# Low parts of the gates' weights: added from DRAM to the negated high part by a GpSimd transfer, instead of subtracted on VectorE

## The chip, the core and the metric

The kernel runs on one core of one Trainium2 chip. The metric is the device time of one execution in microseconds; the time of a kernel is the median of several executions. A core has one instruction queue for each engine, and each engine works its queue in order: PE (TensorE, matrix products, with PEld for the loading of the stationary operand), DVE (VectorE), ACT (ScalarE), POOL (GpSimd) and SP (SyncE, which here only issues transfers). Transfers are carried out by 16 DMA engines.

## What is computed

One layer of a decoder trunk on 512 positions of width 1024, all in float32. The lines below are cut from the reference; attention has three dilated groups, the RWKV-7 mixer has 16 heads of 64, and the feed-forward part has 2816 channels.

```python
h = rms_norm(x, norm1_w[l]) * (1.0 + sc1) + sh1
proj = h @ w_in[l]
att_in, rwkv_in, gate_in = jnp.split(proj, [ATT_IN, ATT_IN + RWKV_IN], axis=-1)
y_att = attention_mixer(att_in) @ w_att_out[l]
y_rwkv = rwkv7_mixer(rwkv_in, ...) @ w_rwkv_out[l]
g_att, g_rwkv = jnp.split(jax.nn.sigmoid(gate_in + b_gate[l]), N_BRANCHES, axis=-1)
x = x + gt1 * ((g_att * y_att + g_rwkv * y_rwkv) @ w_o[l])
h = rms_norm(x, norm2_w[l]) * (1.0 + sc2) + sh2
x = x + gt2 * conv_ffn(h, w_up[l], conv_w[l], conv_b[l], w_down[l])
```

The change touches `gate_in` alone: the last 2048 columns of `w_in` times h, for the two sets of gates.

## The kernel before

**Products.** A float32 matrix product is made of three products of reduced operands (type float32r): each operand is split into a high part, a rounded copy, and a low part, what is left after it. The sum holds high times high, high weights times low input, and low weights times high input. `body` (L1099) makes such a product for 128 columns of weights: kt steps of 128 rows (8 for `w_in`), three products in each. In step k the order is whi with hhi, whi with hlo, wlo with hhi, so the low part of the weights is first read by the third product. A body of eight steps therefore has 24 products of 128x512.

**Weights.** `weights` (L1125) makes the operands of one body: SP loads the 512 KB matrix to `raw`, ACT casts it to `whi` (L1136), DVE subtracts `whi` from `raw` into `wlo` (L1139) and gives `raw` back. There are two buffers of `raw` and two of `whi` and `wlo` (the room "w"), so the cast for a body waits until the body two back has run its last product.

**Gates.** `early_gate` (L1208) is called for 16 blocks of 128 columns (`gate_w`, L1775). Each is a body into the PSUM tile `pg`, followed by a tanh on ACT into `gs` (L1780) and a store of the result to DRAM (`gate_d`), from where it is read back in a later stage.

**Order.** The order on all five engines is fixed when the program is built. `Plan` (L50 to L113) collects tasks, each with an engine, an estimated duration, a priority, the tasks it depends on and the rooms (buffers) it takes and gives back. `run` then plays the plan with these estimates, and always starts the ready task with the lowest priority number on each engine. The engines afterwards follow this order, whatever the real durations are: an engine waits at its next instruction until its inputs are there. `lag` is a time that a task's users wait after the task itself has left its engine, for transfers.

**What stands around the gates.** The RWKV mixer works on four groups of four heads, numbered 0 to 3. Each group goes through two long stages. Its *inverse* inverts triangular blocks: a chain of small DVE operations on the tile `tt` (L1497, L1498, L1505 to L1508) with transposes (L1514, L1519), between which PE has a few `pe` products. Its *chain* runs eight steps over the sequence; in each, PE makes `xy`, ACT copies it to `xs`, PE makes `u`, ACT copies it to `uv`, PE updates, and DVE carries the state `mbd` (L1641), to which POOL has made the decayed state `mp` ahead (L1626). While group g's chain runs, group g+1 is projected (the products `r`, `k`, `v`, whose results are shifted by one position with the help of the ACT copy `sh`, L1147) and goes through its inverse. The products of the gates have the highest priority number of this stage, and so fill what is left between the other products. What fills the end of the last chain is the output product of the attention, `pa`, which opens (`close_pre`, L1079) after all gates are stored.

Of the kernel before, what the change touches and what calls it, by code (L numbers as in the profile page):

```python
# [12 lines left out]
AF = mybir.ActivationFunctionType  # L13
ALU = mybir.AluOpType
# [4 lines left out]
P = 128  # L19
S = 512  # L20
D = 1024
KD = D // P
# [95 lines left out]
C_, E_, W_, V_, I_, M_, S_, U_ = 0.0, 1.0, 2.0, 200.0, 200.15, 220.0, 1.0, 10.0  # L118
# [10 lines left out]
class Layer:  # L129
# [966 lines left out]
    def psx(self, s):  # L1096
        return self.pps.tile([P, 512], F32, tag="px", name=self.n(s), bufs=2)

    def body(self, name, src, kt, room, make, rhs, deps=(), take=(), late=(), last=None, weights=None):  # L1099


        nc, pl = self.nc, self.pl
        n = src.shape[1]
        o = self.bodies = self.bodies + 1
        d = {}
        if weights is None:
            t = self.weights(name, d, src, kt, lambda: self.halves_w(kt, n), W_ + o, deps, tuple(take), ("w",))
        else:
            d["w"], t = None, weights(d, W_ + o)

        def unit(k, j):
            if k == 0 and j == 0:
                d["pm"] = make()
            w, x = d["w"], rhs(k)
            self.mm(d["pm"], w[j // 2][:, k, :], x[j % 2], k == 0 and j == 0, k == kt - 1 and j == 2)
        ends = kt if last is None else last
        for k in range(ends):
            for j in range(3):
                t = pl.add("PE", 0.237, lambda k=k, j=j: unit(k, j), [t] + (list(late) if k + j == 0 else []) +
                           ([self.hk[k]] if j == 0 and rhs == self.hT else []),  # L1120
                           U_ + o, take=(room,) if k + j == 0 else (),
                           give=("w",) if last is None and k == kt - 1 and j == 2 else (), name=name)
        return t, d

    def weights(self, name, d, src, kt, make, prio, deps=(), take=(), buf=()):  # L1125

        nc, pl = self.nc, self.pl
        n = src.shape[1]
        us = kt * n / 1000

        def load():
            d["raw"] = self.load_w(src, kt, n)

        def hi():
            d["w"] = make()
            nc.scalar.copy(d["w"][0], d["raw"])  # L1136

        def lo():
            nc.vector.tensor_tensor(d["w"][1], d["raw"], d["w"][0], op=ALU.subtract)  # L1139
        t = pl.add("DMA", 1.6 * us, load, deps, prio, take=("raw",) + take, lag=2.2, name=name)  # L1140
        t = pl.add("ACT", 0.04 + us, hi, [t], prio, take=buf, name=name + " hi")
        return pl.add("DVE", 0.17 + us / 0.96, lo, [t], prio, give=("raw",), name=name + " lo")

    def shift(self, t, pm, mu, omu, out, take=(), give=(), rows=P, name="shift", deps=()):
# [63 lines left out]
    def early_gate(self, m):  # L1208

        nc, pl = self.nc, self.pl  # L1210
        t, d = self.body("gate", self.gate_w(m), KD, "mm", lambda: self.mmp("pg"), self.hT)

        def tanh():
            d["t"] = self.pp.tile([P, S], F32, tag="km", name=self.n("gs"))
            self.gate(m, d["t"], d["pm"])

        def store():
            self.gd[m] = self.dr.tile([P, S], F32, name=f"gate_d{m}")
            nc.sync.dma_start(self.gd[m], d["t"])
        t = pl.add("ACT", 0.7, tanh, [t, self.pre], E_, take=("km",), give=("mm",))  # L1220
        self.gdt[m] = pl.add("DMA", 0.8, store, [t], M_, give=("km",), lag=2.0, marks=("pre",), name="gate out")
# [916 lines left out]
```

## Time and profile before

| what | value |
|---|---|
| three runs | 1253.78, 1249.96, 1244.15 us; median 1249.96 us |
| the profiled execution's own time | 1247.44 us |
| its span in the profile | 1245.7 us |
| mean granted clock of TensorE in it | 0.984 |
| DMA | 139.39 MB, mean 112 GB/s |
| the chain of work that ended last | PE 82%, DVE 8%, DMA 5%, ACT 2% |

The profile is of one execution. Its page gives busy times of each engine, then the span cut into 40 equal slices of 31.1 us with the busy share of each in tenths, then groups of instructions. In a row, `L1139 DVE` is line and engine, `wlo<-raw,whi` the tile written and the tiles read (buffer numbers left out), and behind the bar stand busy us and mean ns of one. A row of the timeline gives the start in us, the duration, and in square brackets the idle time ahead of it with what ended it. The windows give busy us and the number of instructions of each engine in a stretch. An average over the whole program says little here, since the stages have different limits; the stretch from 410 to 730 us is the one with the inverses, the chains and the gates.

### The profile page before, as it was taken

To read this page: it belongs to the slowest core of one execution; us is meant where nothing else is said; L and a number is where in the kernel's file an instruction comes from. 1 tells how busy PE (TensorE), PEld (TensorE's weight loads), DVE (VectorE), ACT (ScalarE), POOL (GpSimd) and SP (SyncE) were. 2 spreads that over 40 slices of the span, in tenths; PEclk is the share of its full clock that TensorE was granted. 3 is DMA by queue.
4 is the path that set the end of the run, shared out by engine and by line. 5 is a ranking of instruction groups with operands and counts; after the bars stand their busy time and mean duration, and the time that the engine had idled before them with its cause. 6 is when DMAs were issued, how large, how long until landed. Compare 5 with 4: busy or idle time off the path is not lost.

```text
span 1245.7 us, 18047 instructions
## 1 busy us (share of the span) xinstructions
PE 1197.4 (96%) x7012; PEld 976.5 (78%) x7012; DVE 746.5 (60%) x1242; ACT 545.4 (44%) x981; POOL 118.2 (9%) x235
## 2 busy tenths in 40 slices
PE   4999999999999999999999799999999999999997
PEld 3788878888787877777787577788888888878886
DVE  6697862422678968536896844555556566552235
ACT  4484522523566373455445343334443434442133
POOL 4000000000001013030002222214100000000001
PEclk9899999999999999999999789999999999999999
DMA  9745871130333332322330424571133332323331
GB/s 316 242 143 163 274 235 49 46 85 1 92 99 88 97 89 77 110 60 82 92 105 26 146 79 132 174 219 34 56 97 96 90 102 85 102 87 116 102 119 68
DMA packets 168900, 139.39 MB, mean 112 GB/s; under 512 B 8849, under 2 KB 150251, under 8 KB 168815
## 3 DMA queue, kind: packets, MB, share of 16 engines
q1 hardware_dynamic: 168671, 137.98, 36.5%
q8 instruction: 55, 0.90, 0.3%
q14 instruction: 30, 0.25, 0.1%
q10 hardware_dynamic: 144, 0.26, 0.1%
HBM read 127.65 MB, written 10.56 MB: 111 GB/s over the span
## 4 chain that ended last, share of the span: by engine, by line
PE 82%; DVE 8%; DMA 5%; ACT 2%; issue 1%; SPq 0%; POOL 0%; POOLq 0%; DVEq 0%; ACTq 0%
PE u L148 23%; PE o L148 13%; PE v L148 7%; PE pg L148 7%; PE qk L148 6%; PE xy L148 4%; PE pr L148 3%; DMA araw<-in_w_ada_dram 3%; PE k L148 3%; PE pa L148 2%; PE r L148 2%; PE early L148 2%; PE po L148 2%; PE sc L148 1%; PE pt L151 1%
## 5 line engine op out<-in xcount | busy, mean ns | idle before, releaser
L194 DVE TENSOR_TENSOR wlo<-raw,whi 128x1024 fp32r<-128x1024 f32 x67 | 84.1, 1255 | 151.0 <-ACT whi L193 150.9
L148 PE MATMUL u<-h2lo,whi 128*128 128x512 f32 (+2 forms) x368 | 142.3, 387 | 0.0
L148 PE MATMUL u<-h2hi,whi 128*128 128x512 f32 (+2 forms) x368 | 142.3, 387 | 0.0
L148 PE MATMUL u<-h2hi,wlo 128*128 128x512 f32 (+2 forms) x368 | 142.2, 386 | 0.0
L1136 ACT CAST whi<-raw 128x1024 fp32r<-128x1024 f32 (+2 forms) x73 | 72.5, 993 | 130.2 <-PE qk L148 49.5
L193 ACT CAST whi<-raw 128x1024 fp32r<-128x1024 f32 x67 | 70.3, 1049 | 112.0 <-PE o L148 53.8
L1139 DVE TENSOR_TENSOR wlo<-raw,whi 128x1024 fp32r<-128x1024 f32 (+2 forms) x73 | 84.2, 1154 | 22.9 <-ACT whi L1136 22.7
L148 PEld LDWEIGHTS u<-h2hi,wlo 128*128 128x128 f32 x368 | 68.9, 187 | 15.7
L148 PEld LDWEIGHTS u<-h2lo,whi 128*128 128x128 f32 x368 | 68.9, 187 | 15.7 <-POOL h2lo L405 0.2
L148 PEld LDWEIGHTS u<-h2hi,whi 128*128 128x128 f32 x368 | 68.9, 187 | 15.5
L1983 DVE SCALAR_TENSOR_TENSOR u<-u,cols,u 128x511 f32<-128x511 f32 x88 | 65.6, 746 | 4.2 <-ACT u L1981 2.7
L148 PE MATMUL qk<-hhi,wlo 128*128 128x512 f32 x160 | 63.9, 400 | 0.0
L148 PE MATMUL qk<-hlo,whi 128*128 128x512 f32 x160 | 63.6, 397 | 0.0
L148 PE MATMUL qk<-hhi,whi 128*128 128x512 f32 x160 | 63.5, 397 | 0.0
L148 PE MATMUL o<-whi,fhi 128*128 128x512 f32 x144 | 56.1, 390 | 0.3 <-DVE u L1983 0.3
L148 PE MATMUL o<-wlo,fhi 128*128 128x512 f32 x144 | 56.0, 389 | 0.0
L148 PE MATMUL o<-whi,flo 128*128 128x512 f32 x144 | 56.0, 389 | 0.0
L148 PE MATMUL pg<-hhi,wlo 128*128 128x512 f32 x128 | 52.0, 406 | 0.0
L148 PE MATMUL pg<-hlo,whi 128*128 128x512 f32 x128 | 51.8, 405 | 0.0
L148 PE MATMUL pg<-hhi,whi 128*128 128x512 f32 x128 | 51.3, 401 | 0.0
L810 DVE CUSTOM_DVE_ANT_0 sm<-sc,m 128x256 f32<-128x256 f32 (+1 forms) x64 | 24.0, 405 | 37.6 <-PE sc L148 36.5
L347 DVE SCALAR_TENSOR_TENSOR acc<-araw,cols,acc 128x1024 f32<-128x1024 f32 x28 | 35.9, 1282 | 17.2 <-DMA araw<-in_w_ada_dram 17.1
(404 smaller groups left out, 2824.0 us busy)
## 6 DMA issues: line engine op xcount, KB each, us to landing
raw<-in_w_in_dram SPq DMA_DIRECT2D x62, 512.0 KB
raw<-in_w_up_dram SPq DMA_DIRECT2D x44, 512.0 KB
araw<-in_w_ada_dram SPq DMA_DIRECT2D x32, 512.0 KB
raw<-in_w_down_dram SPq DMA_DIRECT2D x22, 512.0 KB
araw<-in_w_ada_dram SPq DMA_DIRECT2D x32, 256.0 KB
wvraw<-in_w_in_dram SPq DMA_DIRECT2D x20, 256.0 KB
gate_d<-gs SPq DMA_DIRECT2D x16, 256.0 KB
gate<-gate_d SPq DMA_DIRECT2D x16, 256.0 KB
```

The costliest lines, as they stand in the source:

```text
L148: return self.nc.tensor.matmul(out, lhsT, rhs, start=start, stop=stop)
L151: self.nc.tensor.matmul(out, in_, self.ident[: in_.shape[0], : in_.shape[0]], is_transpose=True, start=start, stop=stop,)
L193: self.nc.scalar.copy(hl[0], raw)
L194: (lo_eng or self.nc.vector).tensor_tensor(hl[1], raw, hl[0], op=ALU.subtract)
L347: nc.vector.scalar_tensor_tensor(d["acc"], raw, ck, d["acc"], op0=ALU.mult, op1=ALU.add)
L810: nc.vector.tensor_tensor_reduce(d["sm", h][:, :wd], d["sc"][h][:, :wd], m[:, 256 - wd : 256] if gi == 0 else m[:, :wd], 1.0, 3.0e38, op0= ...
L1136: nc.scalar.copy(d["w"][0], d["raw"])
L1139: nc.vector.tensor_tensor(d["w"][1], d["raw"], d["w"][0], op=ALU.subtract)
L1983: nc.vector.scalar_tensor_tensor(u[:, d:], pu[:, : S - d], ch(c), u[:, d:], op0=ALU.mult, op1=ALU.add)
```

## The change

For the 16 gate bodies, and for them alone, the low part is made in another way. `raw` is given back as soon as the cast to `whi` is done. ACT then writes minus `whi` into `wlo`, and POOL issues a transfer that reads the same 512 KB of `w_in` from DRAM once more and adds them to what stands in `wlo`. The subtraction on DVE is gone for these bodies; the other bodies keep it. To the plan, the new ACT task costs what the cast costs, and the POOL task 1.5 us with a lag of 4.0 us.

```diff
@@ body
-    def body(self, name, src, kt, room, make, rhs, deps=(), take=(), late=(), last=None, weights=None):
+    def body(self, name, src, kt, room, make, rhs, deps=(), take=(), late=(), last=None, weights=None, added=False):
...
-            t = self.weights(name, d, src, kt, lambda: self.halves_w(kt, n), W_ + o, deps, tuple(take), ("w",))
+            t = self.weights(name, d, src, kt, lambda: self.halves_w(kt, n), W_ + o, deps, tuple(take), ("w",),
+                             added)
@@ weights
-    def weights(self, name, d, src, kt, make, prio, deps=(), take=(), buf=()):
+    def weights(self, name, d, src, kt, make, prio, deps=(), take=(), buf=(), added=False):
...
         t = pl.add("ACT", 0.04 + us, hi, [t], prio, take=buf, name=name + " hi")
+        if added:
+
+            pl.join([t], give=("raw",))
+            t = pl.add("ACT", 0.04 + us, lambda: nc.scalar.activation(d["w"][1], d["w"][0], AF.Copy, scale=-1.0), [t], prio,
+                       name=name + " neg")
+            return pl.add("POOL", 1.5, lambda: nc.gpsimd.dma_start(
+                d["w"][1], src.rearrange("(k p) f -> p k f", p=P), accum_op=ALU.add), [t], prio, lag=4.0, name=name + " lo")
         return pl.add("DVE", 0.17 + us / 0.96, lo, [t], prio, give=("raw",), name=name + " lo")
@@ early_gate
-        t, d = self.body("gate", self.gate_w(m), KD, "mm", lambda: self.mmp("pg"), self.hT)
+        t, d = self.body("gate", self.gate_w(m), KD, "mm", lambda: self.mmp("pg"), self.hT, added=True)
```

Since the plan is played with other tasks, the order on the engines changes in many places. Line numbers behind L1139 are 7 or 8 higher after the change. In the lists below a row is one instruction in the order of its engine (or several alike, "x4"), with the tile written and the tiles read, their buffer numbers, and the semaphores it waits for.

On ACT at the inverse of group 0, where the first gates are made, `whi_3812` is the high part for the first gate, `whi_3854` (after the change `whi_3856`) that for the second, and the two copies `sh` belong to the projections `r` and `v` of the next group. Before:

```order
L1136 CAST whi_3812<-raw_3668 128x1024 [waits DMAHW2_49,PE_49]
L1147 ACTIVATE sh<-r_3750,cols 128x512 [waits PE_49,Activation_49]
L1136 CAST whi_3854<-raw_3782 128x1024 [waits DMAHW0_49,PE_49]
L1147 ACTIVATE sh<-v_3810,cols 128x512 [waits DVE_49,PE_49]
L1136 CAST whi_3894<-raw_3841 128x1024 [waits DMAHW1_49,DVE_49,PE_49]
```

After:

```order
L1137 CAST whi_3812<-raw_3668 128x1024 [waits DMAHW2_49,PE_49]
L1155 ACTIVATE sh<-r_3750,cols 128x512 [waits PE_49,Activation_49]
L1146 ACTIVATE wlo_3813<-whi_3812 128x1024 [waits Activation_49]
L1137 CAST whi_3856<-raw_3782 128x1024 [waits DMAHW0_49,PE_49]
L1155 ACTIVATE sh<-v_3810,cols 128x512 [waits DVE_49,PE_49]
L1146 ACTIVATE wlo_3857<-whi_3856 128x1024 [waits Activation_49]
L1137 CAST whi_3905<-raw_3825 128x1024 [waits DMAHW1_49,PE_49]
```

The negations stand behind the copies `sh`, and the third cast no longer waits for DVE.

On POOL in the chain of group 0, two steps of the chain (`mp`) with the first operations of an inverse (`tt`) and of the normalization of a chain's output (`var`, `rs`, `yt`). Before:

```order
L1626 TENSOR_SCALAR mp_4400<-mbd_86,pc_3228 128x128 [waits DVE_49]
L1626 TENSOR_SCALAR mp_4400<-mbd_87,pc_3338 128x128
L1486 MEMSET tt_4418 128x512 [waits PE_49,Activation_49]
L1488 TENSOR_SCALAR tt_4418<-rn_4330,half 128x16 [waits Pool_49]
L1488 TENSOR_SCALAR tt_4418<-rn_4330,half 128x16
L1763 TENSOR_SCALAR var_4415<-var_4415 128x4 [waits DVE_49]
L1764 TENSOR_TENSOR rs_4453<-var_4415,mhalf 128x4 [waits Pool_49]
L1765 TENSOR_TENSOR yt_4328<-yt_4328,rs_4453 128x256 [waits Activation_49,Pool_49]
L1626 TENSOR_SCALAR mp_4475<-mbd_86,pc_3228 128x128 [waits DVE_49]
```

After:

```order
L1634 TENSOR_SCALAR mp_4411<-mbd_86,pc_3228 128x128 [waits DVE_49]
L1634 TENSOR_SCALAR mp_4411<-mbd_87,pc_3338 128x128
L1494 MEMSET tt_4432 128x512 [waits Activation_49]
L1496 TENSOR_SCALAR tt_4432<-rn_4300,half 128x16 [waits Pool_49]
L1496 TENSOR_SCALAR tt_4432<-rn_4300,half 128x16
L1148 DMA wlo_4422<-in_w_in_dram 128x8x128 [waits DMASW3_49,PE_49,Activation_49]
L1634 TENSOR_SCALAR mp_4484<-mbd_86,pc_3228 128x128 [waits DVE_49]
```

A gate's transfer now stands between two steps' `mp`, and waits for ACT's negation (and for an earlier transfer and PE).

On PE at the inverse of group 3, which runs beside the chain of group 2: `xy` and `u` belong to that chain, `pe` to the inverse, `pg` are gates, and `t` is a transpose of the chain's output. Before:

```order
L148 MATMUL xy_6652<-uv_6574,gt_5357 64x64 x4
L148 MATMUL u_6161<-xs_6663,gt_5357 64x64 x4
L148 MATMUL xy_6652<-uv_6574,gt_5357 64x64 x4
L148 MATMUL pe_6718<-lt_6408,gt_5848 32x32 x32
L148 MATMUL pe_6718<-tt_6435,lt_6408 32x32 x32
L151 MATMUL t_6808<-ident,yt_6233 128x128
```

After:

```order
L148 MATMUL pg_6579<-hhi,whi_6456 128x512
L148 MATMUL pe_6651<-lt_6309,gt_5757 32x32 x32
L148 MATMUL pg_6579<-hlo,whi_6456 128x512
L148 MATMUL pg_6579<-hhi,wlo_6457 128x512
L148 MATMUL pg_6690<-hhi,whi_6589 128x512
L148 MATMUL pg_6690<-hlo,whi_6589 128x512
L148 MATMUL pg_6690<-hhi,wlo_6590 128x512
L148 MATMUL pg_6690<-hhi,whi_6589 128x512
L148 MATMUL pg_6690<-hlo,whi_6589 128x512
L148 MATMUL pe_6651<-tt_6350,lt_6309 32x32 x32
```

Before, the gates were all done when this inverse came to its products; after the change the last two gates run around them. Between the first product of group 2's inverse and the first of group 3's, PE has 80 gate products before the change and 111 after it.

## What I expected, on record before the run

> **What bounds the kernel now.** I read the page's busy times and its 40 slices first, then the windows of the stretch in which the sixteen gate products run, then single instructions there.
>
> ```profile
> span 1245.7 us, 18047 instructions
> PE 1197.4 (96%) x7012; PEld 976.5 (78%) x7012; DVE 746.5 (60%) x1242; ACT 545.4 (44%) x981; POOL 118.2 (9%) x235
> PE   4999999999999999999999799999999999999997
> DVE  6697862422678968536896844555556566552235
> PEclk9899999999999999999999789999999999999999
> ```
>
> PE is full but for the start, the end and slice 23 (around 700 us), where its granted clock dips too. DVE has spare time on the whole, but is nearly full in a few slices. The windows of the stretch show which (columns: busy us and instructions of PE, PEld, DVE, ACT, POOL, then clock, DMA share, GB/s):
>
> ```profile
> 419.00:434.20 15.20, 15.05 (x67) 12.13 (x65) 14.64 (x23) 5.58 (x8) 0.00 (x0) 1.00 0.50 138
> 442.00:494.00 52.00, 52.00 (x432) 40.54 (x431) 35.62 (x84) 28.69 (x65) 13.28 (x26) 1.00 0.26 77
> 494.00:513.00 19.00, 19.00 (x204) 15.36 (x203) 15.95 (x23) 8.17 (x11) 3.52 (x3) 1.00 0.49 146
> 631.00:651.00 20.00, 20.00 (x206) 16.36 (x205) 19.32 (x27) 10.94 (x15) 0.66 (x1) 1.00 0.39 104
> 651.00:696.00 45.00, 44.43 (x367) 33.93 (x366) 31.06 (x76) 20.88 (x50) 11.94 (x24) 1.00 0.13 41
> 696.00:727.00 31.00, 21.47 (x238) 17.53 (x239) 23.04 (x40) 14.24 (x30) 4.81 (x7) 0.56 0.60 183
> ```
>
> The inverses (DVE's long chains) run in 419 to 434, 494 to 513, 631 to 651 and 680 to 707. In the first three PE is full, because gate products fill it; in the fourth the gate products are used up, PE does 21.47 us of work in 31 us, and the clock falls to 0.56. So a us taken from DVE is worth something only at 696 to 727. Everywhere else PE sets the pace, and what counts is whether a gate's weights are there when PE gets to them. The time after is therefore the time before, plus new PE waits, less what of that one gap is filled.
>
> **Removed and added work, by engine.**
>
> ```profile
> L1139 DVE TENSOR_TENSOR wlo<-raw,whi 128x1024 fp32r<-128x1024 f32 x28 | 34.2, 1221 | 9.0 <-ACT whi L1136 8.9
> L1136 ACT CAST whi<-raw 128x1024 fp32r<-128x1024 f32 x28 | 29.4, 1049 | 53.6 <-PE pg L148 21.9 <-PE k L148 13.7 <-PE r L148 7.7
> ```
>
> Sixteen subtractions of 1.221 us leave DVE: 19.5 us, none of it on PE's path but in the gap. Sixteen negations come to ACT. The nearest row is the cast of the same size, 1.05 us, so 16.8 us; ACT is busy 5.58 of 15.2 us and 28.69 of 52 in the windows above, so the load fits, and I cost it only as latency of the weights. Should that cover go, each negation could hold a chain's copy by up to 1.05 us. The raw buffer is given back after the cast instead of the subtraction, which lets SP's next load go some 1.2 us or more earlier; PE doesn't wait for raw, so that is worth nothing. DMA gets 16 x 512 KB more to read, in windows that are at most 0.6 busy.
>
> **The price of the accumulating transfer, D.** No row shows one, nor any transfer issued by POOL.
>
> ```profile
> 575.22 3.92 DMA raw<-in_w_in_dram
> L1764 POOL TENSOR_TENSOR rs<-var,mhalf 128x4 f32<-128x4 f32 x16 | 16.5, 1030 | 1.3
> L1875 POOL TENSOR_TENSOR gate<-gate,gate 128x512 f32<-128x512 f32 x8 | 11.2, 1403 | 45.0 <-DVE gate L1874 45.0
> ```
>
> The same matrix loaded plainly by SP takes 3.92 us to land. At 146 GB/s for a share of 0.49 (494 to 513) full DMA moves 298 GB/s, so the 512 KB take 1.76 us of it, and 2.16 us are fixed. Lower end: 3.92, if adding costs nothing and POOL issues as fast as SP; a gain over the plain load has no reason, since the same bytes come from the same place. Upper end: two plain transfers in a row and POOL's longest row of this size, 2 x 3.92 + 1.40 = 9.2. I take 2.16 + 2 x 1.76, since the tile is read as well as the matrix, plus 1.03 for POOL writing the request: D = 6.7, nearer the middle than either end.
>
> **New waits on PE.** Before, a gate's low part follows its high part on DVE. Now it is cast, negation and D, and the cast waits as before until PE has finished the body two back.
>
> ```profile
> 413.69 1.05 ACT L1136 CAST whi<-raw 128x1024 fp32r<-128x1024 f32 x1 [2.14 <-PE r L148]
> 414.64 0.68 ACT L1147 ACTIVATE sh<-r,cols 128x512 f32<-128x512 f32 x1
> 418.93 0.19 PEld L148 LDWEIGHTS pg<-hhi,whi 128*128 128x128 f32 x1
> 632.23 0.69 ACT L1147 ACTIVATE sh<-r,cols 128x512 f32<-128x512 f32 x1
> 631.29 5.44 PE v L148 x24
> 502.37 0.68 ACT L1780 ACTIVATE gs<-pg,b_gate 128x512 f32<-128x512 f32 x1
> 645.80 1.13 PE pe L148 x64
> 498.26 0.58 PE t L151 x4
> ```
>
> A body is 24 products in 5.44 us, 0.227 each; only its third product reads the low part, so 0.45 us of each wait is covered.
> (a) First gate at inverse 0. The negation stands behind the copy sh: it ends at 414.64 + 0.68 + 1.05 = 416.4, the transfer lands at 423.1, PE is free at 418.93: 4.2 - 0.45 = 3.7.
> (b) First gate at the third inverse (inverse 2), the same way: 632.23 + 0.69 + 1.05 + 6.7 = 640.7 against 636.73: 4.0 - 0.45 = 3.5.
> (c) Third gate at inverse 0: cast 1.05, tanh 0.68, negation 1.05, hops some 0.15, D, together 9.65, from the end of the first gate; PE has 24 products and two inverse products, 5.44 + 2 x 1.13 = 7.7: 1.9 - 0.45 = 1.5.
> (d) The last two gates of the first chain: 9.65 again, against 5.44 + 2.1 of chain products, and against 5.44 + 2 x 0.58: 1.6 and 2.6, together 4.2.
> In the chains a body lasts about 5.44 + 5 = 10.5 us, because a chain's own products stand between; 9.65 fits, so nothing there.
>
> **The gap, and what takes its place.**
>
> ```profile
> 706.42 0.71 DVE L1519 STREAM_TRANSPOSE lt<-tt 128x512 f32<-128x512 f32 x1
> 707.19 1.94 PE pe L148 x64
> 701.59 1.11 PE L148 MATMUL u<-xs,gt 64*64 64x64 f32 x8 [0.51 <-ACT xs L1621]
> 720.21 2.00 PE pa L148 x4
> 723.68 1.99 PE t L148 x4
> 688.53 0.68 PE L148 MATMUL u<-xs,gt 64*64 64x64 f32 x8
> ```
>
> Now about 31 more gate products (7.0 us) run after the third inverse, around the fourth one's products, and DVE has five subtractions less there. That fills 31 - 21.47 = 9.5 us of idle time. The clock stays up, too: two inverse products at 1.13 instead of 1.94 (1.6), pa and t x4 at 0.91 instead of 2.00 and 1.99 (2.2), and four groups of eight like u at 0.68 instead of 1.11 (1.7), about 6 after rounding up for smaller ones; it could be 0 or, at (1 - 0.56) x 21.47, 9.4. Gain: 15.5. Next is late the last chain: in its new order two steps stand with no other product between, and two nearly so.
>
> ```profile
> 686.80 0.67 PE L148 MATMUL xy<-uv,gt 64*64 64x64 f32 x8
> 687.57 0.37 ACT L1621 COPY xs<-xy 64x256 f32<-64x256 f32 x1 [2.33 <-PE xy L148]
> 689.24 0.37 ACT L1658 COPY uv<-u 64x256 f32<-64x256 f32 x1 [1.30 <-PE u L148]
> 684.52 0.61 DVE L1641 SCALAR_TENSOR_TENSOR mbd<-u,pc,mp 128x128 f32<-128x128 f32 x2
> 685.23 0.72 POOL L1626 TENSOR_SCALAR mp<-mbd,pc 128x128 f32<-128x128 f32 x2 [2.36 <-DVE mbd L1641]
> 692.23 0.61 DVE L1641 SCALAR_TENSOR_TENSOR mbd<-u,pc,mp 128x128 f32<-128x128 f32 x2 [1.20 <-ACT uv L1590]
> ```
>
> In a bare step PE waits for two copies and the carry, 0.37 + 0.37 + 0.61, and some six hops of 0.1, less the 0.67 us of its output products that fit in: 1.3. (e) 2 x 1.3 + 2 x 0.5 = 3.6.
>
> **Sum.** 3.7 + 3.5 + 1.5 + 4.2 + 3.6 - 15.5 = +1.0 us. The profiled execution took 1247.44 us (span 1245.7), 0.2% under the median of the three runs, 1249.96; added to the median: 1251.
>
> POOL's queue: six of its transfers stand ahead of an mp of a chain. mp ends at 685.95 and is read at 692.23, some 6 us later, so a hold of POOL below about 5 us is covered; the mp behind waits for the negation too.
>
> **Rivals.** They differ in D, whose slope is about 5 us per us.
> *Slow transfer, slower.* At D = 9.2: (a) 6.2, (b) 6.0, (c) 4.0, (d) 4.1 + 5.1, (e) 3.6, and four bodies in chains fall short by 12.15 - 10.5 - 0.45 = 1.2 each: 33.8 - 15.5 = +18, 1268. Over 1% slower from D = 8.4 on. For it: the transfer is of 512-byte pieces, two reads for one write. Against: DMA is at most half busy there.
> *Hidden transfer.* At D = 3.92: 0.9 + 0.7 + 0 + 0 + 3.6 - 15.5 = -10, 1240; with the last chain filled, too, -14, 1236, which is faster by over 1%. For it: the plain load. [...]
> *POOL held, slower.* If writing the request holds POOL for 7.5 us, six mp are late by 2.5 each, and D grows by as much as POOL is held beyond 1.03: over 1270, in any case. [...]
> *The relief isn't used.* If the gap stays as it is and the waits come on top: 16.5, 1266.
>
> **How the numbers follow.** About 1% is what a measurement of this kernel tells from no change (the three runs differ by 0.8%). My case, D from 4.5 to 8.4: 0.48. Hidden transfer: 0.16, of it 0.10 faster by over 1%. Slow transfer 0.25, POOL held 0.06, relief unused 0.05: slower 0.36. So faster 0.10, same 0.54, slower 0.36. Range: 1238 leaves out about 0.08 below; above, D could exceed my bound, and 1281 (about D = 11) leaves out 0.12.
>
> **What would show it.** Right: PE waits for wlo at its first gates of inverses 0 and 2 by 3 to 4 us each, the window of 31 us is full and its clock near 1, DVE has 19.5 us less, and the last chain shows gaps of half a us. Wrong: a wlo that lands over 8 us after POOL's issue, PE waits inside the chains, mp late, or the clock falling at the new waits.

## The result, and the profile after

The changed kernel takes 1255.75 us (median of 6 runs, 1255.32 to 1262.1) against 1249.1 us before: a ratio of 1.0064, 95% interval 1.0038 to 1.0090. It is slower by 0.6%, clear of the scatter but within the 1% that the prediction took as no change, and 4.75 us above the 1251 that was predicted. The profiled execution took 1255.35 us.

The page of the changed kernel, busy times and three of its rows of slices:

```profile
span 1253.6 us, 18111 instructions
PE 1202.6 (96%) x7012; PEld 978.1 (78%) x7012; DVE 726.2 (58%) x1226; ACT 560.3 (45%) x997; POOL 142.1 (11%) x251
PE   4999999999999899999989989999999999999997
DVE  6697862422678948436975745555555565552235
PEclk9899999999999999999989979999999999999999
```

DVE has lost its 20 us and ACT gained 15. The dip of PE and its clock that stood in slice 23 is gone; PE has new ones in slices 14, 21 and 24, the clock in the last two of them. The windows of the same stretches as before show them (busy us of PE, PEld, DVE, ACT, POOL, then clock, DMA share, GB/s):

```profile
419.00:434.20 15.20, 11.77 (x111) 9.30 (x110) 13.97 (x21) 8.22 (x12) 3.07 (x2) 1.00 0.93 159
494.00:513.00 19.00, 16.86 (x194) 12.69 (x192) 14.24 (x22) 8.67 (x13) 4.33 (x5) 1.00 0.70 153
631.00:651.00 20.00, 16.48 (x177) 12.78 (x176) 16.31 (x25) 8.09 (x11) 2.94 (x2) 0.83 0.70 121
696.00:727.00 31.00, 30.47 (x340) 23.65 (x338) 19.29 (x34) 15.41 (x33) 8.38 (x11) 1.00 0.36 76
727.00:773.00 46.00, 42.90 (x295) 33.80 (x294) 19.96 (x38) 20.96 (x48) 14.92 (x22) 0.81 0.49 148
```

The window of the fourth inverse, 696 to 727, is now full at full clock, as forecast. The first three inverses, which were full before, are now short of it by 3.4, 2.1 and 3.5 us of PE, and the last chain (727 to 773, 46.00 of 46 before) by 3.1 us and a fifth of its clock. The transfers, from the list of DMA issues (the last number is the median from issue to landing):

```profile
wlo<-in_w_in_dram POOLq DMA_DIRECT2D x16, 512.0 KB, 6.7
```

And from the instructions of their line (shortest, median and longest on POOL, in ns):

```profile
L1148 POOL DMA_DIRECT2D wlo<-in_w_in_dram x16: 1522/1600/1788, 416.8 to 703.8; - x16
```

The timeline has five waits of PE for a landing, and six waits in the last chain, of which two are shown; what ended the idle time stands in brackets:

```profile
423.36 0.50 PE L148 MATMUL pg<-hhi,wlo 128*128 128x512 f32 x1 [3.43 <-DMA wlo<-in_w_in_dram]
438.58 0.50 PE L148 MATMUL pg<-hhi,wlo 128*128 128x512 f32 x1 [1.34 <-DMA wlo<-in_w_in_dram]
495.82 0.50 PE L148 MATMUL pg<-hhi,wlo 128*128 128x512 f32 x1 [0.85 <-DMA wlo<-in_w_in_dram]
504.01 0.50 PE L148 MATMUL pg<-hhi,wlo 128*128 128x512 f32 x1 [1.02 <-DMA wlo<-in_w_in_dram]
637.32 0.79 PE L148 MATMUL pg<-hhi,wlo 128*128 128x512 f32 x1 [3.52 <-DMA wlo<-in_w_in_dram]
...
725.36 0.45 PE L148 MATMUL u<-uv,bkt 128*64 128x64 f32 x8 [0.46 <-ACT uv L1666]
730.45 0.68 PE L148 MATMUL u<-xs,gt 64*64 64x64 f32 x8 [1.22 <-ACT xs L1629]
```

Between the first product `r` of group 0 and the first product of the feed-forward part the profiles take 529.2 us before and 536.7 after. Summed over windows of 2.5 us there, PE is idle 15.3 us before and 19.9 after, and loses 9.4 and 10.7 us to the clock (busy time times one minus the clock). Each of these is one execution.

### The profile page after: what moved, and what is told of

It reads as the page before. It is cut to its first block, busy times and chain, and to the rows that moved or that the text cites. A ratio compares the mean times of both kernels' runs of the same rounds, so it can differ in the third digit from the quotient of the medians.

```text
span 1253.6 us, 18111 instructions
## 1 busy us (share of the span) xinstructions
PE 1202.6 (96%) x7012; PEld 978.1 (78%) x7012; DVE 726.2 (58%) x1226; ACT 560.3 (45%) x997; POOL 142.1 (11%) x251
## 4 chain that ended last, share of the span: by engine, by line
PE 78%; DMA 9%; DVE 7%; ACT 3%; issue 2%; SPq 1%; POOL 0%; POOLq 0%; DVEq 0%; ACTq 0%
PE u L148 23%; PE o L148 11%; PE v L148 8%; PE pg L148 7%; PE qk L148 6%; PE xy L148 4%; PE r L148 3%; PE k L148 3%; PE pa L148 2%; DMA araw<-in_w_ada_dram 2%; DMA wlo<-in_w_in_dram 2%; PE early L148 2%; PE po L148 2%; DMA raw<-in_w_o_dram 2%; PE sc L148 1%
## 5 line engine op out<-in xcount | busy, mean ns | idle before, releaser
L148 PEld LDWEIGHTS u<-h2hi,wlo 128*128 128x128 f32 x368 | 68.9, 187 | 15.5
L1140 DVE TENSOR_TENSOR wlo<-raw,whi 128x1024 fp32r<-128x1024 f32 (+2 forms) x57 | 64.1, 1129 | 27.5 <-ACT whi L1137 27.5
L148 PE MATMUL pg<-hhi,wlo 128*128 128x512 f32 x128 | 54.0, 422 | 10.2 <-DMA wlo<-in_w_in_dram 10.2
```

Of the source, the lines that this page charges most:

```text
L148: return self.nc.tensor.matmul(out, lhsT, rhs, start=start, stop=stop)
```

## The experiments

The question was why the filled gap brought nothing. Two accounts stood against each other. By the first, each wait for `wlo` is a loss of its own (10.2 us in the trace), added to a real gain. By the second, the loss lies in the order: the plan counts on a late low part and so puts fewer gate products ahead of the first inverses, where PE then stands still whether the low part is late or not. Each ratio below is to the kernel before, on the same chip; the last three experiments ran on another chip than the rest, on which the kernel before takes 1248.46 us. The edits are cut to the lines that matter. Those of the relief alone, the transfer in the order of before, the subtraction on POOL and the order of the last five gates are shown against the kernel before (`added` marks the gate bodies, as in the change), the others against the changed kernel.

**The transfer left out, same order.** The product of `wlo` reads the bare negation.

```diff
-            return pl.add("POOL", 1.5, lambda: nc.gpsimd.dma_start(
-                d["w"][1], src.rearrange("(k p) f -> p k f", p=P), accum_op=ALU.add), [t], prio, lag=4.0, name=name + " lo")
+            return pl.add("POOL", 1.5, lambda: None, [t], prio, lag=4.0, name=name + " lo")
```

> The transfer is left out; the order of every engine stays that of the change, and the products read the bare negation (the low part is left out of the sum). Theory W (the loss is the time from the negation to the landed low part): the five waits of PE for wlo, 10.2 us, go, and the clock's dip at 635 to 650 us (about 3 us) goes with the longest of them: 1255.8 - 10.2 - 3.0 = 1242.6, between 1240 and 1246. Theory O (the loss is in the new order and in ACT's negations): the waits go, but other waits take their place, and it stays above 1250.

Measured: 1254.83 us, 1.0056 (1.0035 to 1.0077). Theory W falls: the 10.2 us of waits are gone, but PE's idle time between the two marks named above is 18.0 us, against 19.9 in the change. The largest group of PE's waits in this kernel (us in all, times, longest):

```profile
PE pe L148 <- DVE lt L1526: 6.6, 3, 3.2
```

And two of them in its timeline:

```profile
435.10 1.85 PE L148 MATMUL pe<-lt,gt 32*32 32x32 f32 x64 [3.20 <-DVE lt L1526]
651.20 1.92 PE L148 MATMUL pe<-lt,gt 32*32 32x32 f32 x64 [3.08 <-DVE lt L1526]
```

No wait for `wlo` is left, and PE stands at the same two inverses for DVE's `lt` instead, for almost as long. The changed kernel shows why, in DVE's and PE's rows at the first and the third inverse:

```profile
430.38 0.71 DVE L1527 STREAM_TRANSPOSE lt<-tt 128x512 f32<-128x512 f32 x1
431.51 1.20 PE L148 MATMUL pe<-lt,gt 32*32 32x32 f32 x64
...
642.69 0.71 DVE L1527 STREAM_TRANSPOSE lt<-tt 128x512 f32<-128x512 f32 x1
647.01 1.20 PE L148 MATMUL pe<-lt,gt 32*32 32x32 f32 x64
```

At the first inverse `lt` was ready at 431.09 and PE came at 431.51. Had PE not waited 3.43 us for `wlo`, it would have waited about 3 us for `lt`; only 0.4 us of that wait was a loss. At the third, where the clock fell too (0.58 from 636 to 640 us), `lt` was ready at 643.40 and PE came 3.6 us later; by these rows that much was lost there. The time doesn't show this gain of some 4 us: it is 0.9 us lower. In the profiled execution without the transfer the clock fell at both waits for `lt` (the 64 products behind them took 1.85 and 1.92 us, against 1.20 in the changed kernel), and the loss to the clock is 15.5 us instead of 10.7; the rest wasn't traced.

**The transfer sent where nobody reads it, same order.** Its target is a tile in DRAM, which one more transfer fills ahead.

```diff
+        self.scr = self.dr.tile([P, KD, P], F32, name="scr")
+        self.nc.gpsimd.dma_start(self.scr, self.w_in[0][:, :P].rearrange("(k p) f -> p k f", p=P))
...
             return pl.add("POOL", 1.5, lambda: nc.gpsimd.dma_start(
-                d["w"][1], src.rearrange("(k p) f -> p k f", p=P), accum_op=ALU.add), [t], prio, lag=4.0, name=name + " lo")
+                self.scr, src.rearrange("(k p) f -> p k f", p=P), accum_op=ALU.add), [t], prio, lag=4.0, name=name + " lo")
```

> Each transfer is issued at its old place on POOL, with the same reads and the add, but into a tile in DRAM that no product reads (the low part is left out of the sum). Theory W: as without a transfer, 1242.6, at most 2 us more. Theory T (POOL, held 1.6 us by each issue, and the doubled DMA traffic cost the time): as the change, 1254 to 1257, with waits for mp or for raw.

Measured: 1256.57 us, 1.0064 (1.0041 to 1.0087). The time is the one that T gave, but not for T's reason: no wait for `mp` or `raw` came, the waits are those of the kernel without transfer (6.9 us for `lt`), and the two intervals overlap for the most part (the medians differ by 1.7 us). POOL is held longer here than in the change, since it waits 25.0 us in four places for the transfer before into the same tile. So POOL's issues and the traffic cost nothing that is clear of the scatter.

**The transfer without its add.**

```diff
-                d["w"][1], src.rearrange("(k p) f -> p k f", p=P), accum_op=ALU.add), [t], prio, lag=4.0, name=name + " lo")
+                d["w"][1], src.rearrange("(k p) f -> p k f", p=P)), [t], prio, lag=4.0, name=name + " lo")
```

> The transfer of the change without its add, so that wlo is overwritten by the weights (the low part is wrong by that). By the sum of the prediction the add is one share of 1.76 us in 6.7: a transfer lands 4.9 us after its issue, the waits of PE fall from 3.4, 1.3, 0.9, 1.0 and 3.5 to 1.7, 0, 0, 0 and 1.7, together by 6.8: 1249, or 1246 if the clock's dip goes too. Rival: the add is free and the time lies in POOL's issue and the way: the landing stays at 6.7 us and the time at 1255 to 1257.

Measured: 1251.22 us, 1.0031 (1.0009 to 1.0053). The same two rows as above for this kernel, of the DMA issues and of the line on POOL:

```profile
wlo<-in_w_in_dram POOLq DMA_DIRECT2D x16, 512.0 KB, 5.0
```

```profile
L1148 POOL DMA_DIRECT2D wlo<-in_w_in_dram x16: 873/970/1122, 419.3 to 704.1; - x16
```

The add costs 1.7 us of 6.7, of which 0.63 is POOL's longer issue. Waits for `wlo` fell from 10.2 us to 3.3, and waits for `lt` rose from none to 2.9. The add isn't free, as the rival had it. The time is even 3.6 us below that of the kernel without any transfer, at the edge of the scatter. At the first inverse PE waits here 1.65 us for `wlo` and then 1.28 for `lt`, where that kernel waited 3.20 in one piece, and 1.61 and 1.21 at the third; the profile loses 9.5 us to the clock, that one 15.5. That two short waits spare the clock is a reading of these two profiles and was not tested by itself.

**The order of the change, the work back on DVE.**

```diff
-            return pl.add("POOL", 1.5, lambda: nc.gpsimd.dma_start(
-                d["w"][1], src.rearrange("(k p) f -> p k f", p=P), accum_op=ALU.add), [t], prio, lag=4.0, name=name + " lo")
+            return pl.add("POOL", 1.5, lambda: nc.vector.tensor_tensor(
+                d["w"][1], d["w"][1], d["w"][0], op=ALU.add), [t], prio, lag=4.0, name=name + " lo")
```

> The order of the change on PE, ACT and SP, but at the transfer's place in the plan DVE makes one operation of two inputs and the same size on wlo (the low part is left out of the sum), so DVE gets back its sixteen operations of 1.2 us. Theory F (the gap at the fourth inverse is filled by the order alone, since gate products stand there now): as without a transfer, 1242 to 1247. Theory R (DVE's relief fills it): DVE's inverses are late again by up to 19.5 us in all, PE waits for lt and gt at the fourth inverse again, and it takes 1250 or more.

Measured: 1262.48 us, 1.0111 (1.0081 to 1.0140): the time that R gave, but not at the place it gave. The inverses in its timeline:

```profile
435.08 1.92 PE L148 MATMUL pe<-lt,gt 32*32 32x32 f32 x64 [5.34 <-DVE lt L1527]
514.56 1.20 PE L148 MATMUL pe<-lt,gt 32*32 32x32 f32 x64 [0.35 <-DVE lt L1527]
654.29 1.40 PE L148 MATMUL pe<-lt,gt 32*32 32x32 f32 x64 [3.87 <-DVE lt L1527]
718.37 1.20 PE L148 MATMUL pe<-lt,gt 32*32 32x32 f32 x64
```

At the fourth inverse PE doesn't wait, though DVE has all its work back: the order alone fills that gap, as F had it. But R's waits for `lt` came too, at the first and third inverses, where this order has taken the filler away. In this order DVE's relief is worth 7.7 us (1262.48 against 1254.83), part of which may be that five of the sixteen operations hold up DVE for ACT's negation, 6.8 us in all.

**The plan told that there is no transfer.** The same work as in the first experiment, in an order of its own.

```diff
-            t = pl.add("ACT", 0.04 + us, lambda: nc.scalar.activation(d["w"][1], d["w"][0], AF.Copy, scale=-1.0), [t], prio,
-                       name=name + " neg")
-            return pl.add("POOL", 1.5, lambda: nc.gpsimd.dma_start(
-                d["w"][1], src.rearrange("(k p) f -> p k f", p=P), accum_op=ALU.add), [t], prio, lag=4.0, name=name + " lo")
+            return pl.add("ACT", 0.04 + us, lambda: nc.scalar.activation(d["w"][1], d["w"][0], AF.Copy, scale=-1.0), [t], prio,
+                       name=name + " neg")
```

> No transfer, and the plan knows it: a gate's weights are ready with the negation, so the plan puts 50 gate products ahead of the first inverse's products instead of the change's 37 (the low part is left out of the sum). Theory O (the loss of the change is that its plan, which counts on a late low part, takes gate products away from the first three inverses, where PE then waits, for wlo or for DVE's inverse, whichever ends last): the idle time of PE in the stretch of the gates falls from 13.6 us to 2 to 5, and the kernel takes 1236 to 1244, faster than before. Rival L (the relief of DVE isn't worth anything in any order): 1247 to 1255.

Measured: 1246.71 us, 0.9972 (0.9958 to 0.9986), between both theories' numbers. It says two things. The same instructions in two orders differ by 8.1 us (1254.83 and 1246.71), which is more than the whole loss of the change; in the two profiles PE's idle time between the marks is 18.0 and 12.6 us, and the loss to the clock 15.5 and 12.1. And a low part that costs DVE and DMA nothing at all wins 0.3% in the order that this plan makes of it.

**The relief alone, in the order of before.** The third product reads `whi`.

```diff
+        if added:
+            return pl.add("DVE", 0.17 + us / 0.96, lambda: None, [t], prio, give=("raw",), name=name + " lo")
...
-            self.mm(d["pm"], w[j // 2][:, k, :], x[j % 2], k == 0 and j == 0, k == kt - 1 and j == 2)
+            self.mm(d["pm"], w[0 if added else j // 2][:, k, :], x[j % 2], k == 0 and j == 0, k == kt - 1 and j == 2)
```

> The kernel before with its own order on every engine, but the sixteen subtractions of the gates are left out, and the third product reads the high part (the low part is left out of the sum). It shows the relief of DVE by itself. Theory O: PE was full at the first three inverses, so nothing is won there, and at the fourth only what brings the inverse's start forward: 1243 to 1249. Rival R (the relief is worth most of the gap, as the prediction had it): 1233 to 1240.

Measured: 1247.17 us, 0.9993 (0.9974 to 1.0011): no difference that can be told. The fourth inverse in its timeline:

```profile
709.66 1.92 PE L148 MATMUL pe<-lt,gt 32*32 32x32 f32 x64 [3.46 <-DVE lt L1522]
712.98 1.23 PE L148 MATMUL pe<-tt,lt 32*32 32x32 f32 x38 [1.41 <-ACT lt L1563]
716.39 1.09 PE L151 MATMUL t<-ident,yt 128*128 128x128 f32 x4 [1.49 <-DVE gt L1565]
```

The gap stands there as in the kernel before, whose rows are:

```profile
707.19 1.92 PE L148 MATMUL pe<-lt,gt 32*32 32x32 f32 x64 [2.92 <-DVE lt L1519]
710.51 1.92 PE L148 MATMUL pe<-tt,lt 32*32 32x32 f32 x64 [1.41 <-ACT lt L1560]
713.91 1.09 PE L151 MATMUL t<-ident,yt 128*128 128x128 f32 x4 [1.49 <-DVE gt L1562]
```

The sixteen subtractions weren't what made the fourth inverse late.

**The transfer in the order of before.** The plan takes negation and transfer for a cast and a subtraction, so that PE's order is that of before to the last product.

```diff
             nc.scalar.copy(d["w"][0], d["raw"])
+            if added:
+                nc.scalar.activation(d["w"][1], d["w"][0], AF.Copy, scale=-1.0)
...
+        if added:
+            return pl.add("DVE", 0.17 + us / 0.96, lambda: nc.gpsimd.dma_start(
+                d["w"][1], src.rearrange("(k p) f -> p k f", p=P), accum_op=ALU.add), [t], prio, give=("raw",),
+                name=name + " lo")
```

> The negation and the transfer of the change, in the order of before on PE, DVE and SP (the plan takes them to be as quick as a subtraction; raw is given back as before). Now the 64 gate products at the first inverse all stand ahead of its own products. Theory O: the waits for wlo are real there, about 3.4 us for the first gate and 3.9 for the third at the first inverse, the same at the third inverse, and 2 to 4 for each gate at the ends of the chains: 1262 to 1275. Rival W (the waits cost the same in both orders, and the order of the change loses by itself): 1252 to 1258.

Measured: 1283.25 us, 1.0271 (1.0228 to 1.0314), above what O gave. PE's waits for the landing, all together (us, times, longest):

```profile
PE pg L148 <- DMA wlo<-in_w_in_dram: 21.9, 8, 5.3
```

The longest stands right behind the third inverse, in the timeline:

```profile
690.31 0.80 PE L148 MATMUL pg<-hhi,wlo 128*128 128x512 f32 x1 [5.26 <-DMA wlo<-in_w_in_dram]
```

In the old order the waits for `wlo` are real, and the gap at the fourth inverse is still there. The new order of the change saves 27.5 us against this one. It is the better answer to a late low part, and itself costs 8.

**The subtraction on POOL.** It keeps DVE free without a transfer, as the attempt at a version that beats both.

```diff
+            return pl.add("POOL", 2.7, lambda: nc.gpsimd.tensor_tensor(d["w"][1], d["raw"], d["w"][0], op=ALU.subtract),
+                          [t], prio, give=("raw",), name=name + " lo")
```

> The whole computation, with the gates' subtraction on POOL (2.7 us each by the plan) in place of negation and transfer: DVE is relieved as by the change, and the low part is ready some 3 us after the cast instead of 8.7. Theory O: 1238 to 1246, faster than before. Rival P (POOL's mp of the chains stand behind the subtractions, or POOL and DVE slow each other at the inverses): 1249 to 1258, with waits of PE for mp or mbd, or longer DVE operations beside POOL's.

Measured: 1264.64 us, 1.0123 (1.0081 to 1.0164). DVE is busy 748.4 us, 22 more than after the change with the same instructions. Rows of POOL and of DVE at the first inverse:

```profile
417.15 2.50 POOL L1144 TENSOR_TENSOR wlo<-raw,whi 128x1024 fp32r<-128x1024 f32 x1 [14.69 <-ACT whi L1137]
417.43 0.57 DVE L1511 TENSOR_REDUCE tt<-tt 128x20 f32<-128x400 f32 x1
418.04 1.65 DVE L1512 SCALAR_TENSOR_TENSOR tt<-tt,sup 128x10 f32<-128x10 f32 x1
...
421.64 0.24 DVE L1512 SCALAR_TENSOR_TENSOR tt<-tt,sup 128x11 f32<-128x11 f32 x1
...
422.59 2.39 POOL L1144 TENSOR_TENSOR wlo<-raw,whi 128x1024 fp32r<-128x1024 f32 x1 [2.94 <-ACT whi L1137]
423.51 1.51 DVE L1512 SCALAR_TENSOR_TENSOR tt<-tt,sup 128x12 f32<-128x12 f32 x1
```

An operation of 0.24 us (as at 421.64, with no work of POOL beside it) lasts until POOL's subtraction ends: 418.04 + 1.65 = 419.69 against 417.15 + 2.50 = 419.65, and 425.02 against 424.98. Rival P was right by its second half, and the time lies above its range. Its first half isn't seen: DVE has no wait for `mp` in this trace. How much of the 15 us comes from DVE's longer operations and how much from the order of this kernel's own plan isn't separated.

**Only the order of the last five gates.** Subtraction on DVE as before; the plan alone counts on 6 us more.

```diff
+        if added:
+            t = pl.add("DVE", 0.17 + us / 0.96, lo, [t], prio, give=("raw",), name=name + " lo")
+            return pl.add("DMA", 0.0, lambda: None, [t], prio, lag=6.0)
...
-        t, d = self.body("gate", self.gate_w(m), KD, "mm", lambda: self.mmp("pg"), self.hT)
+        t, d = self.body("gate", self.gate_w(m), KD, "mm", lambda: self.mmp("pg"), self.hT, added=m >= 11)
```

> The kernel before, subtraction on DVE for all gates, no transfer and no negation; only the plan is told that the last five gates' weights take 6 us more. By its order 29 gate products move away from ahead of the third inverse's products (75 to 46) and 31 come ahead of the fourth's (72 to 103). Theory S (gate products are a fixed supply, and what fills one inverse opens another): the idle time at the fourth inverse goes (about 9.7 us, with its low clock), PE waits 4 to 7 us for DVE's lt at the third inverse, and the time stays within 1244 to 1252. Rival G (the gap at the fourth inverse is worth 15 us to whatever fills it): 1233 to 1240.

Measured: 1249.82 us, 1.0016 (0.9999 to 1.0034). The third and the fourth inverse:

```profile
645.41 1.91 PE L148 MATMUL pe<-lt,gt 32*32 32x32 f32 x64 [6.33 <-DVE lt L1523]
711.73 1.92 PE L148 MATMUL pe<-tt,lt 32*32 32x32 f32 x64 [2.77 <-ACT lt L1564]
```

The window of the fourth inverse, first before, then in this kernel:

```profile
690.00:727.00 37.00, 27.10 (x287) 21.74 (x286) 27.67 (x50) 16.94 (x36) 7.00 (x10) 0.63 0.50 153
```

```profile
690.00:727.00 37.00, 30.87 (x329) 24.30 (x328) 26.68 (x49) 17.40 (x38) 7.84 (x10) 0.86 0.43 128
```

Theory S holds in the time and at the third inverse: what was taken from there opened 6.33 us. At the fourth it holds in part. The idle time fell from 9.9 us to 6.1, where S had it go, and the clock rose from 0.63 to 0.86. Rival G falls.

**The change for the last five gates alone.** Negation and transfer as in the change.

```diff
-        t, d = self.body("gate", self.gate_w(m), KD, "mm", lambda: self.mmp("pg"), self.hT, added=True)
+        t, d = self.body("gate", self.gate_w(m), KD, "mm", lambda: self.mmp("pg"), self.hT, added=m >= 11)
```

> The change for the last five gates alone (negation and transfer); the first eleven keep their subtraction. 52 products stand ahead of the third inverse and 97 ahead of the fourth. These five gates run between steps of the third chain, where the change showed no wait for wlo. Theory S: as the order alone, 1244 to 1252. Rival W (the loss of the change is its waits at the first gates, and the rest of it wins): 1236 to 1243.

Measured: 1249.47 us, 1.0005 (0.9987 to 1.0024), as S had it. One wait of 3.66 us for `wlo` stands at 645.18, where the third inverse of the order alone waited 6.33 for `lt`; the expectation had no wait at these gates.

**The plan told the measured landing.**

```diff
-                d["w"][1], src.rearrange("(k p) f -> p k f", p=P), accum_op=ALU.add), [t], prio, lag=4.0, name=name + " lo")
+                d["w"][1], src.rearrange("(k p) f -> p k f", p=P), accum_op=ALU.add), [t], prio, lag=5.2, name=name + " lo")
```

> The change, but the plan is told the measured 6.7 us from issue to landing (1.5 and a lag of 5.2 in place of 4.0). By its order 32 products stand ahead of the first inverse instead of 37, and 48 instead of 19 come after the fourth. Theory S: PE's waits for wlo fall from 10.2 us to below 7, its waits at the inverses and in the last chain grow by as much, and the time stays within 1253 to 1261. Rival W: the waits for wlo are the loss, and it takes 1246 to 1252.

Measured: 1258.56 us, 1.0077 (1.0059 to 1.0096). PE waits 7.6 us for `wlo`, 2.6 less than in the change, and in its chains 6.7 us for `xs` and `uv`, 1.8 more. That is the direction of S, though the waits for `wlo` stayed above its 7 us. An exact price in the plan doesn't help.

Counted from the order, the gate products between the first products of successive inverses, and then up to the first `pa`, are:

| kernel | to 1st | to 2nd | to 3rd | to 4th | to `pa` | median us |
|---|---|---|---|---|---|---|
| before | 65 | 156 | 83 | 80 | 0 | 1249.1 |
| the change | 37 | 142 | 68 | 111 | 26 | 1255.75 |
| no transfer, new plan | 50 | 133 | 100 | 101 | 0 | 1246.71 |
| last five late, order alone | 65 | 156 | 54 | 109 | 0 | 1249.82 |
| landing as measured | 32 | 106 | 79 | 113 | 54 | 1258.56 |

Each row adds up to 384. (The expectations of the last three experiments count between other marks, so their numbers differ from these by some units.) This is the explanation that the experiments support: gate products are a fixed supply, and what fills one inverse is missing at another, where PE then waits for DVE. The counts alone don't give the times; those depend on the waits and on the clock as well.

## Why the prediction came out as it did

The time lies within the range and within 1% of before, the case forecast as likeliest; it is 4.75 us above the number.

- **The transfer.** 6.7 us was forecast and 6.7 measured. The parts were off: POOL's issue is 1.60 us, not 1.03, and the add is 1.1 us of the way, not a second 1.76. The two errors cancel, so the exact hit is luck.
- **The waits.** (a) 3.7 became 3.43, (b) 3.5 became 3.52, (c) 1.5 became 1.34, (e) 3.6 became 3.57 (six waits in the last chain). (d), the last gates of the first chain, was 4.2 and became 0.85 + 1.02 = 1.9.
- **The gap.** Its idle time was forecast at 9.5 us; the waits of before from 696 to 719 us add up to 9.75, and none is left there. The mechanism given for it was half wrong. "DVE has five subtractions less there" is not what fills it: with the subtractions gone and the order kept, the gap stood, and with the order changed and DVE's work back, it was filled.
- **The clock: this is the step of the sum that failed.** "The clock stays up, too ... about 6" was counted as a gain. In the trace the loss to the clock went from 9.4 us to 10.7, and over more executions the mean granted clock hardly moved: its median is 0.983 in 21 executions of the kernel before and 0.984 in the six of the changed one. The low clock left 700 to 725 us (0.50 before, 1.00 after) and came back at two other places: after wait (b), and in the bare last chain, where no filler stands until `pa` opens. The windows of the changed kernel there:

```profile
636.00:640.00 4.00, 2.68 (x6) 2.15 (x7) 3.86 (x7) 0.00 (x0) 1.55 (x1) 0.58 1.11 204
...
735.00:740.00 5.00, 4.18 (x29) 3.54 (x30) 1.37 (x4) 1.56 (x4) 0.83 (x2) 0.50 0.90 267
```

With the measured terms the sum is 3.43 + 3.52 + 1.34 + 1.9 + 3.57 - 9.75 + 1.3 = +5.3 us, against a difference of 6.65 in the medians and of 7.5 in the profiles. Of the 2.2 us that are left in the profiles, 0.6 is other idle time of PE (in all it grew by 4.6, by these terms 4.0) and 1.6 is longer busy time of PE, which wasn't traced further. Against the forecast of +1.0 the clock is 7.3 us off and (d) 2.3 us the other way, so the number came as near as it did partly by luck.

- **Adding the waits up.** The sum comes near, but its terms aren't causes that can be taken away one by one. The experiments split the change differently: a free low part with its own plan, -2.4 us (1249.16 to 1246.71); the order that a late low part makes the plan choose, +8.1; the transfer itself with all its waits, +0.9 (1254.83 to 1255.75, which is within the scatter).
- **The rivals.** The slow and the hidden transfer fell with the measured 6.7 us. POOL held fell with the unread transfer. "The relief isn't used" came nearest, though its condition, a gap that stays, didn't come: DVE's relief buys nothing in the old order, and in the new one only mends what that order opens.
- **The signs.** All the signs named for "right" came, and so did two of those for "wrong": the clock fell at a new wait, (b), and the slowest of the 16 transfers landed 8.7 us after its issue. The range, 1238 to 1281, would have held every experiment but one, so that the time lies in it says little of the mechanism.

Why the clock fell at one wait and not at another of the same length is open.

## What to carry to other kernels

Where a planner sets the order, an operand's estimated latency moves work before its real latency stalls anything: count the filler ahead of each waiting point in both orders, and treat it as a fixed supply. Before a wait is priced as a loss, ask what the waiting engine would wait for next at that place; take the cause away in the same order, and then in a new plan, and the two differences tell waits from order. A gap filled is a gain only if the filler didn't stand somewhere useful.

## What the runs showed of the hardware

**The clock after a wait.** At the first inverse the changed kernel waited 3.43 us, and the kernel with the longer lag 3.47 us, at the same product. The windows behind it, first of the one, then of the other:

```profile
424.00:428.00 4.00, 4.00 (x19) 3.31 (x18) 3.79 (x7) 0.00 (x0) 0.00 (x0) 1.00 1.15 149
```

```profile
424.00:428.00 4.00, 4.00 (x14) 3.21 (x13) 3.79 (x7) 0.00 (x0) 0.00 (x0) 0.70 1.18 147
```

One kept its clock at 1.00, the other was granted 0.70. In the last chain of the changed kernel the clock stood at 0.50 from 735 to 740 us with PE busy 4.18 of 5 us and no wait longer than 1.22 us since the gates ended; the products there are small ones of 64x64, 128x64 and 128x128. It was low in these two windows as well, the first of the kernel without the transfer, the second of the one with the transfer in the order of before:

```profile
650.00:651.00 1.00, 0.00 (x0) 0.00 (x0) 0.97 (x2) 0.56 (x1) 0.00 (x0) 0.64 0.59 175
```

```profile
429.00:432.00 3.00, 3.00 (x9) 2.32 (x8) 2.86 (x5) 0.00 (x0) 0.00 (x0) 0.51 1.19 148
```

The first lies inside the wait of 3.08 us shown above, which began at 648.12: the clock was down at 0.64 before PE had been idle for 2.9 us. The second lies behind a wait of 2.94 us that ended at 427.02, with PE at work again for 2 us, and the clock was 0.51. In the kernel before, the clock fell from 1.00 to 0.61 between 698 and 699 us and to 0.50 behind it, with no wait around it longer than 1.71 us. So in these executions the clock was low at waits of 3.08 and 2.94 us and stayed at 1.00 behind one of 3.43: the length of a wait alone doesn't tell here what it costs.

**POOL against DVE.** In the kernel with the subtraction on POOL, two DVE operations with two tiles as inputs that began beside it ended with it, at 1.65 and 1.51 us instead of 0.24, while a reduction (one input) beside it took 0.57 us, as long as the same one in the changed kernel.
